# One transformer layer in float32 on one core: the first feed-forward product written out in seven slots, and parts of the output projection issued later

## The chip, the core and the metric

The kernel runs on one core of a Trainium2 chip. A core has five engines with an instruction stream each: TensorE (PE: matmuls, with a weight load of its own, PEld), VectorE (DVE), ScalarE (ACT), GpSimd (POOL) and SyncE (SP), which here issues the transfers to and from DRAM. The metric is device time in microseconds (us), the median of several runs. Each engine works through its own stream in order; semaphores hold an instruction until what it reads is written and what it overwrites has been read.

## The reference

One layer over x of 512 x 2048 float32: a norm, a combined projection to queries, keys and values, two kinds of attention with 8 heads each, an output projection, and a feed-forward block with 8192 hidden columns. Cut to what matters here:

```python
x = x + einsum('bse,ed->bsd', mixed, w_out)          # output projection
h2 = rmsnorm(x, g_mlp)
u = relu(einsum('bsd,df->bsf', h2, w_up))            # first feed-forward product
x = x + einsum('bsf,fd->bsd', u * u, w_down)         # second feed-forward product
return rmsnorm(x, g_final)
```

## The kernel before

**Two halves of a number.** A float32 operand is split into a high part that TensorE takes at full speed (fp32r) and a low part, the rest: ScalarE casts (L65, `CAST`), VectorE subtracts (L66). This pair is called a split here; `split` keeps the last of each as `casts` and `lows`. A matmul of two split operands takes three or four passes.

**Seven products in place of eight.** Each large product is cut into 2 x 2 blocks and done with seven block products, numbered 1 to 7, after Strassen and Winograd. The price is sums of blocks before a product (the parts of an operand, such as b22 - b12) and after it (the closes).

**Attention's end and the output projection (up to about 801 us).** `left(p, j)` splits part j of the left operand (the attention output `mixed`) for product p into `ah` and `al`, some parts with a sum on VectorE (L281 to L287). `split` with a scale does the values of attention, `vh` and `vl` (L68, L69). The last heads' probabilities are split into `ph` and `pl`. Products run in the order 1, 6, 2, 5, 3, 6 (last quarter), 7, 4, each in column halves c and steps j. The adds of their results into the residuals r are at L595. TensorE's order is written by hand from product 2 on; the other engines' order is made by a scheduler that goes by its own costs.

**The turn (about 780 to 830 us).** The results are transposed on TensorE (`turn_block`, the transposes at L681), scaled into `h`, summed and split into the seven forms fh1 to fh7 and fl1 to fl7 (`to_sum`, `to_high`, `to_low`).

**The first feed-forward product (about 801 to 1448 us).** It goes over 32 units of 256 hidden columns. A unit has seven products of sixteen matmuls: eight of 128x512 (L912) with the high part of the weights, eight of 128x256 (L914) with the low part, accumulated in three banks of PSUM, psa, psb and psc. Products 1, 6, 7 and 4 use psa, 2 uses psb, and 5 and 3 use psc. `split_part(p)` splits the weights of product p (`wu` to `wh` and `wl`). `close(p)` takes a result out: ScalarE copies psa to s (L925) for 1, 6 and 7 or to c (L941) for 4, and VectorE adds (L932 to L944). After product 3 ScalarE applies Relu and Square (L946, L947). Products of two units are interleaved: while unit u does 1, 5, 6, 2, 7, unit u - 1 ends with 4 and 3.

The weights' sums t1, t2, t3 (parts 5, 6 and 7) are for 20 of the 32 units made earlier in the program and stored in DRAM (`td`; the list `early`). The other 12 make their own: three sums of 128x1024 on VectorE (L890 to L893), from the raw weights. Part 4 always needs one more sum (L898).

**Stores.** Two units make a pair. When the odd one has its Square, the pair's seven parts for the second feed-forward product are made by `store_form`: for parts 5, 6, 7 and 3 a sum on VectorE (L661 to L667), then for each part a cast on ScalarE and a low on VectorE (`st`), then a store of 512 KB. Up to four are written per unit. The tiles of st rotate.

Of the kernel before, what the change touches and what calls it, by code (L numbers as in the profile page):

```python
# [8 lines left out]
F32 = mybir.dt.float32  # L9
# [31 lines left out]
def block_kernel(ctx, tc, x, g_attn, w_in, b_f, g_out_sb, g_out_fox, w_out, g_mlp, w_up, w_down, g_final, y):  # L41
# [18 lines left out]

    lows, casts, loads, scaled = [None], [None], [None], [None]

    def split(hi, lo, src, scale=None):
        if scale is None:
            ins = casts[0] = act.copy(hi, src)  # L65
            lows[0] = dve.tensor_tensor(lo, src, hi.bitcast(F32), op=ALU.subtract)  # L66
        else:
            ins = act.mul(hi, src, scale)  # L68
            scaled[0] = dve.scalar_tensor_tensor(lo, src, scale, hi.bitcast(F32), op0=ALU.mult, op1=ALU.subtract)  # L69
        return ins  # L70
# [138 lines left out]
    with tc.tile_pool(name="att", bufs=1, side="right") as at:  # L209
# [61 lines left out]
        def left_tile(p, pool_):  # L271
            LT[p] = tuple(pool_.tile([P, NH, 2 * P], F32R, tag=f"f{q}{LEFT_AT[p]}", name=f"a{q}{p}") for q in "hl")

        def left(p, j, k=1):

            m0, m1 = late["mixed"]
            ks = slice(2 * j, 2 * (j + k))
            a11, a21, a12, a22 = (m[:, ks, i:i + 2 * P] for m in (m0, m1) for i in (0, 2 * P))
            s = late["s"][j] if p in (5, 6, 3) else None
            if p == 5:  # L280
                dve.tensor_tensor(s, a21, a22, op=ALU.add)  # L281
            if p == 6:
                dve.tensor_tensor(s, s, a11, op=ALU.subtract)
# [213 lines left out]
        with tc.tile_pool(name="attp", bufs=1, space=PSUM) as atp:  # L497
# [58 lines left out]
            def before_outputs():  # L556
                late["mixed"] = [mixp.tile([P, NH, NT], F32, tag=f"x{i}", name="mixed") for i in range(2)]
                for k in range(2 * NH - 4):
                    load_mixed(k)
                left(1, 0)  # L560
                left(1, 1)

            def first_outputs():
# [11 lines left out]
                late["s"] = [w.rearrange("p (a b) -> p a b", a=2) for c in range(2) for w in two(c)]  # L575
# [185 lines left out]
    for c in range(2):  # L761
        for j in range(4):
            run_all(out_product(C[c], 5, c, [j], True, False))
            if j % 2:
                left(7, 2 * c + j // 2)
        add(r22[c], C[c])
# [43 lines left out]
    for j in range(4):  # L810
# [28 lines left out]
    class Unit:  # L839
        def __init__(self, u):  # L840
# [7 lines left out]

            def blocks():
                return rw.tile([P, 2, KC // 2, P], F32, tag="rw", name="wu")  # L850

            def wide(src):
                raw = rw.tile([P, KC // 2, 2 * P], F32, tag="rw", name="wu")
                sp.dma_start(raw, src)
                return [raw[:, :, j * P:(j + 1) * P] for j in range(2)]

            r, q = blocks(), blocks()
            b11, t2, t1, t3 = r[:, 0], r[:, 1], q[:, 0], q[:, 1]
            sp.dma_start(b11, first[:, :, :P])
            self.raw = u not in early  # L860
            if self.raw:
                sp.dma_start(t1, first[:, :, P:])
                sp.dma_start(t3, last[:, :, P:])
                sp.dma_start(t2, last[:, :, P:])
            else:
                for t_, j in ((t1, 0), (t2, 2), (t3, 1)):
                    sp.dma_start(t_, td[u][:, j])
            b21, b22 = wide(last)
            self.b = {1: b11, 5: t1, 6: t2, 2: b21, 7: t3, 3: b22, 4: b21}
            self.open_banks()  # L870

# [15 lines left out]
        def split_part(self, p):  # L887
            hi, lo = (w.rearrange("p (a b) -> p a b", b=P) for w in hi_lo(2 * NT))
            if p == 5 and self.raw:
                dve.tensor_tensor(self.b[7], self.b[7], self.b[5], op=ALU.subtract)  # L890
                dve.tensor_tensor(self.b[5], self.b[5], self.b[1], op=ALU.subtract)
            if p == 6 and self.raw:
                dve.tensor_tensor(self.b[6], self.b[6], self.b[5], op=ALU.subtract)  # L893
            if p == 4 and self.u < 2:
                dve.tensor_tensor(self.b[4], self.b[4], self.b[6], op=ALU.subtract)
            split(hi, lo, self.b[p])
            if p == 2 and self.u > 1:
                dve.tensor_tensor(self.b[4], self.b[4], self.b[6], op=ALU.subtract)  # L898
            self.parts[p] = hi, lo

        def product(self, p):
            if p not in self.parts:
                self.split_part(p)
            self.multiply(p)
            self.close(p)

        def multiply(self, p):
# [8 lines left out]
        def close(self, p):  # L916
# [26 lines left out]
            if p == 3:  # L943
                dve.tensor_tensor(self.m6, self.m6, self.C, op=ALU.add)  # L944
                sums(self.c[:, 1, t1], self.m6)
                act.activation(self.c, self.c, AF.Relu)  # L946
                act.activation(self.c, self.c, AF.Square)  # L947

# [101 lines left out]
    add(r21[0], A[0])  # L1050
    ahead[2] = out_piece(4, 1, 2)
    out_step(1)
    ahead[3] = out_piece(4, 1, 3)
    u0, u1 = Unit(0), Unit(1)
    u0.more(5)
    turn_block(1, 0, r21[0])
    to_sum(5, 0)
# [10 lines left out]
    u0.split_part(2)  # L1068
    u0.more(7)
    to_high(6, 0)  # L1070
# [13 lines left out]
    u1.split_part(1)  # L1084
    u1.more(5)
    for n in (1, 3):
# [25 lines left out]
    u1.multiply(2)  # L1112
    u0.split_part(7)
    for n in (0, 2):
# [5 lines left out]
    u0.multiply(5)  # L1120
    u1.split_part(5)
    both_cm.__exit__(None, None, None)
# [13 lines left out]
    u1.others()  # L1136
    for who, p in ((u0, 6), (u0, 7), (u1, 5), (u1, 6), (u0, 4), (u1, 7), (u0, 3)):
        who.product(p)
    more_parts.append(parts_hx)
    out_cm.__exit__(None, None, None)  # L1140
    old = u1
    for u in range(2, NU + 1):
        new = Unit(u) if u < NU else None
        if u == NU - 1:
            for p in ORDER:
                load_uf(p, GROUPS[0])
            b_first = load_b(GROUPS[0], 0)
        if new is None:
            second(1, b_first, 0, GROUPS[0][1], True)
        for i, (who, p) in enumerate(((new, 1), (old, 4), (new, 5), (new, 6), (old, 3), (new, 2), (new, 7))):  # L1150
            if who is None:
                continue
            who.product(p)
            if u == 3 and p == 6:
                v2 = cp.tile([P, TB], F32, name="v2")
                dve.tensor_reduce(v2, ss2, axis=mybir.AxisListType.X, op=ALU.add)
                dve.tensor_scalar(v2, v2, 1.0 / D, EPS, op0=ALU.mult, op1=ALU.add)
                ev = cp.tile([P, TB], F32, name="ev")
                dve.scalar_tensor_tensor(ev, v2, EPS, v2, op0=ALU.mult, op1=ALU.mult)
            if todo and u < NU - 1 and i in (0, 2, 4, 5):  # L1160
                store_form(*todo.pop(0))
            if p == 3 and who.u % 2 == 1 and who.u < NU - 2:
                todo += [(q, who.pair, who.u - 1) for q in A_ORDER]
        old = new
# [160 lines left out]
```

## Time and profile before

| | |
|---|---|
| time, median of 3 runs | 2074.25 us (2071.03 to 2074.33) |
| profiled execution | 2072.78 us, span 2071.1 us |
| TensorE busy | 2036.7 us, 98% |
| VectorE busy | 1656.5 us, 80% |
| ScalarE busy | 1074.2 us, 52% |
| mean granted TensorE clock | 0.996 |

A row of a time line gives the start, the duration, the engine, the line of the kernel, the operation with its tiles (written <- read) and shapes, and in brackets how long the engine had idled and what released it. A row of a group gives the count, then the busy time and the mean in ns, then the idle time before such instructions and what ended it. A row of the waits gives the total, the number and the longest. A row of the windows gives the busy time of each engine with its number of instructions, then the granted clock, the busy share of the DMA engines and GB/s. Busy times overlap: an instruction can start before the one ahead of it on its engine has ended, so the distance from start to start is what one costs in a row.

### The profile page before, as it was taken

How to read it: one execution, taken by the hardware profiler on the slowest of the kernel's cores; microseconds unless marked ns; L12 is line 12 of the kernel's file. 1: busy time of each engine (PE TensorE's matmuls, PEld its weight loads, DVE VectorE, ACT ScalarE, POOL GpSimd, SP SyncE). 2: the span in 40 equal slices, each digit the busy share in tenths (PEclk: the TensorE clock that was granted, in tenths of full speed). 3: DMA queues.
4: the chain of work that ended last, by engine and by line, in shares of the span. 5: the costliest groups of instructions: out<-in, count | busy, mean ns of one | idle time of the engine just before them, and what ended most of it. 6: DMA issues, size and time to landing. Idle time of an engine off the chain costs nothing.

```text
span 2071.1 us, 26773 instructions
## 1 busy us (share of the span) xinstructions
PE 2036.7 (98%) x10188; PEld 1729.7 (84%) x10188; DVE 1656.5 (80%) x1866; ACT 1074.2 (52%) x1419; POOL 69.7 (3%) x73
## 2 busy tenths in 40 slices
PE   9999999999999999999999999999999999999998
PEld 8888888888887888888888888888888888888886
DVE  4767767768777778888888888887899989888886
ACT  5334334444546566666666666655744434443433
POOL 0000000001102000000000000000000000000003
PEclk9999999999999999999999999999999999999999
DMA  7888878888754876776877777777865764764722
GB/s 242 270 292 280 287 251 272 287 274 265 254 187 140 257 231 197 255 251 232 268 247 241 257 261 254 235 248 261 293 244 215 268 242 159 267 236 131 269 93 102
DMA packets 371728, 492.60 MB, mean 238 GB/s; under 512 B 12760, under 2 KB 258568, under 8 KB 362512
## 3 DMA queue, kind: packets, MB, share of 16 engines
q1 hardware_dynamic: 370640, 488.77, 71.2%
q10 hardware_dynamic: 960, 2.13, 0.3%
q8 instruction: 80, 1.31, 0.2%
q14 instruction: 48, 0.39, 0.1%
HBM read 373.39 MB, written 117.46 MB: 237 GB/s over the span
## 4 chain that ended last, share of the span: by engine, by line
PE 88%; DVE 5%; DMA 3%; ACT 2%; issue 1%; SPq 0%; ACTq 0%; DVEq 0%
PE psa L912 9%; PE accd L99 8%; PE accd L98 8%; PE accd L100 8%; PE accq L98 5%; PE accq L99 5%; PE accq L100 5%; PE psa L914 5%; PE psc L912 5%; PE accv L98 3%; PE accv L99 3%; PE accv L100 3%; PE psc L914 2%; PE psb L912 2%; DMA ufd<-st 2%
## 5 line engine op out<-in xcount | busy, mean ns | idle before, releaser
L65 ACT CAST wh<-wraw 128x1024 fp32r<-128x1024 f32 (+2 forms) x157 | 160.8, 1026 | 241.8 <-PE accq L99 113.4
L66 DVE TENSOR_TENSOR wl<-wraw,wh 128x1024 fp32r<-128x1024 f32 (+2 forms) x157 | 186.7, 1191 | 101.0 <-ACT wh L65 100.7
L65 ACT CAST wh<-wu 128x1024 fp32r<-128x1024 f32 x160 | 166.9, 1049 | 116.4 <-PE psa L912 48.0
L65 ACT CAST wh<-wd 128x1024 fp32r<-128x1024 f32 (+1 forms) x134 | 132.6, 999 | 181.4 <-PE accd L100 125.0
L66 DVE TENSOR_TENSOR wl<-wu,wh 128x1024 fp32r<-128x1024 f32 x160 | 194.5, 1221 | 27.8 <-ACT wh L65 21.8
L98 PE MATMUL accq<-hH,wh 128*128 128x512 f32 x512 | 201.1, 393 | 0.0
L100 PE MATMUL accq<-hH,wl 128*128 128x512 f32 x512 | 199.8, 390 | 0.0
L99 PE MATMUL accq<-hL,wh 128*128 128x512 f32 x512 | 199.6, 390 | 0.0
L66 DVE TENSOR_TENSOR wl<-wd,wh 128x1024 fp32r<-128x1024 f32 (+1 forms) x134 | 153.1, 1153 | 34.9 <-ACT wh L65 34.7
L98 PE MATMUL accd<-wh,uf 128*128 128x512 f32 x428 | 166.5, 389 | 0.1
L100 PE MATMUL accd<-wh,uf 128*128 128x512 f32 x428 | 166.5, 389 | 0.0
L99 PE MATMUL accd<-wl,uf 128*128 128x512 f32 x428 | 166.5, 389 | 0.0
L65 ACT CAST wx<-wd 128x1024 fp32r<-128x1024 f32 (+1 forms) x90 | 89.5, 1001 | 118.3 <-PE accd L100 79.1
L66 DVE TENSOR_TENSOR wx<-wd,wx 128x1024 fp32r<-128x1024 f32 (+1 forms) x90 | 103.1, 1155 | 21.7 <-ACT wx L65 21.6
L99 PE MATMUL accd<-wx,uf 128*128 128x512 f32 x292 | 114.0, 390 | 0.5 <-DVE wx L66 0.3
L98 PE MATMUL accd<-wx,uf 128*128 128x512 f32 x292 | 113.6, 389 | 0.2 <-ACT wx L65 0.2
L100 PE MATMUL accd<-wx,uf 128*128 128x512 f32 x292 | 113.6, 389 | 0.0
L100 PEld LDWEIGHTS accq<-hH,wl 128*128 128x128 f32 x512 | 96.1, 188 | 20.1
L99 PEld LDWEIGHTS accq<-hL,wh 128*128 128x128 f32 x512 | 96.2, 188 | 19.0
L98 PEld LDWEIGHTS accq<-hH,wh 128*128 128x128 f32 x512 | 96.2, 188 | 18.9
L1020 DVE TENSOR_TENSOR m<-m,accd 128x1024 f32<-128x1024 f32 x84 | 102.2, 1217 | 11.1 <-PE accd L100 11.1
L912 PE MATMUL psa<-fh,wh 128*128 128x512 f32 x392 | 106.6, 394 | 0.7 <-ACT s L925 0.7
(307 smaller groups left out, 4845.4 us busy)
## 6 DMA issues: line engine op xcount, KB each, us to landing
ufd<-st SPq DMA_DIRECT2D x98, 512.0 KB, 5.4
wd<-in_w_down_dram SPq DMA_DIRECT2D x48, 1024.0 KB, 7.2
wraw<-in_w_in_dram SPq DMA_DIRECT2D x84, 512.0 KB, 5.8
uf<-ufd SPq DMA_DIRECT2D x42, 1024.0 KB, 6.6
wu<-in_w_up_dram SPq DMA_DIRECT2D x66, 512.0 KB, 6.8
wu<-in_w_up_dram SPq DMA_DIRECT2D x32, 1024.0 KB, 8.5
sums<-in_w_up_dram SPq DMA_DIRECT2D x60, 512.0 KB, 5.3
td<-sums SPq DMA_DIRECT2D x20, 1536.0 KB, 5.8
```

The lines of the kernel that those rows point to most:

```text
L65: ins = casts[0] = act.copy(hi, src)
L66: lows[0] = dve.tensor_tensor(lo, src, hi.bitcast(F32), op=ALU.subtract)
L98: pe.matmul(out, sh, mh, start=first, stop=False, skip_group_check=True)
L99: pe.matmul(out, sh, ml, start=False, stop=False, skip_group_check=True)
L100: pe.matmul(out, sl, mh, start=False, stop=last, skip_group_check=True)
L912: pe.matmul(ps, hi[:, a, :], both, start=a == 0 and p in (1, 2, 5), stop=False, skip_group_check=True)
L914: pe.matmul(ps[:, :2 * P], lo[:, a, :], F[p][a // 4][:, a % 4, 0, :], start=False, stop=a == KC // 2 - 1, skip_group_check=True)
L1020: dve.tensor_tensor(M[p][:, :, db, :], M[p][:, :, db, :], ps, op=ALU.add)
```

## The change

1. **The unit loop.** Its body is written out in seven slots, one for each product on TensorE, in the order new 1, new 5, old 4, new 6, old 3, new 2, new 7 (before, as written: new 1, old 4, new 5, new 6, old 3, new 2, new 7, with TensorE's order left to the scheduler). The order of ScalarE and VectorE is now the written one for units 2 to 30. Each split is written three slots ahead of its product.
2. **Stores.** In even steps one store form, in odd steps six.
3. **Own sums.** `early` is now every even unit and 1, 5, 21 and 31; again 20 units. The units that make their own sums are 3, 7, 9, 11, 13, 15, 17, 19, 23, 25, 27 and 29, so these sums stand in even steps, a unit ahead. The loads of a unit are three pieces (`load_r`, `load_q`, `load_wide`) in three of its slots.
4. **The output projection.** `left_after` issues a part after the last cast and the last low. The sums s of parts 0 and 1 are made earlier, and the other parts are spread over later steps. `left(1, 2, 2)` waits for both instructions of the last scaled split.
5. **The turn.** One more piece of product 4 goes ahead, the block's turn stands before `out_step(1)`, and the first units' products go 6, then unit 1's 5, then 7.

The number of instructions on each engine stays the same; their order and the rotation of their tiles differ.

The diff, cut to its core:

```diff
-    early = [u for u in range(NU) if u % 8 not in (2, 5, 7)]
+    early = [u for u in range(NU) if u % 2 == 0 or u in (1, 5, 21, 31)]
...
+        def left_after(*what):
+            with tc.issue_after(casts[0].ins), tc.issue_after(lows[0].ins):
+                left(*what)
...
-                with tc.issue_after(scaled[0].ins):
+                with tc.issue_after(scaled[0].ins), tc.issue_after(scaled[1].ins):
                     left(1, 2, 2)
...
-                        if c == 0 and j < 3:
-                            left(5, j)
-                            left(6, j)
+                        if j < 3:
+                            left_after(6 if c else 5, j)
...
-                        if c == 0 and j == 0:
-                            left(2, 0, 2)
-                        if c == 0 and j == 1:
-                            left(2, 2)
+                        if c == 1 and j == 0:
+                            left_after(2, 0, 2)
+                        if c == 1 and j == 1:
+                            left_after(2, 2)
...
-    ahead = {j: out_piece(4, 1, j) for j in range(2)}
+    ahead = {j: out_piece(4, 1, j) for j in range(3)}
...
+    FORMS = [(0, 1, 0, 0, 0, 0), (1, 1, 1, 1, 1, 1)]
...
+    rows_cm = tc.manual_schedule(engines={act.engine, dve.engine})
+    rows_cm.__enter__()
...
+    for u in range(2, NU - 1):
+        old, new = units_[u - 1], units_[u]
+        nxt = units_[u + 1] = Unit(u + 1)
+        odd = u % 2
+        nxt.load_r()
...
+        new.multiply(1)
+        if u > 2:
+            old.close(7)
+        store_next(FORMS[odd][0])
+        new.split_part(6)
+        new.multiply(5)
+        new.close(1)
+        old.split_part(3)
+        nxt.load_q()
+        store_next(FORMS[odd][1])
+        old.multiply(4)
+        new.split_part(2)
+        new.last_sum()
+        nxt.load_wide()
+        store_next(FORMS[odd][2])
+        new.multiply(6)
+        old.close(4)
+        new.split_part(7)
+        store_next(FORMS[odd][3])
+        old.multiply(3)
+        new.close(6)
+        nxt.split_part(1)
+        nxt.raw_sum(7)
+        store_next(FORMS[odd][4])
+        new.multiply(2)
+        old.close(3)
+        nxt.raw_sum(5)
+        nxt.split_part(5)
+        old.square()
+        store_next(FORMS[odd][5])
+        if old.u % 2 == 1 and old.u < NU - 2:
+            todo += [(q, old.pair, old.u - 1) for q in A_ORDER]
+        new.multiply(7)
+        new.close(2)
+        new.split_part(4)
+        nxt.raw_sum(6)
...
-    for u in range(2, NU + 1):
-        new = Unit(u) if u < NU else None
...
-        for i, (who, p) in enumerate(((new, 1), (old, 4), (new, 5), (new, 6), (old, 3), (new, 2), (new, 7))):
...
-            if todo and u < NU - 1 and i in (0, 2, 4, 5):
-                store_form(*todo.pop(0))
```

**VectorE at the end of attention.** w is an attention score tile (its scan is at L400 before and L404 after), al and wl are lows of the left parts and of the weights, vl the low of the values. Before, from the last scan to the fourth vl:

```order
L400 SCALAR_TENSOR_TENSOR w_5219<-w_5219 128x128
L66 TENSOR_TENSOR al5_5323<-r_5314,ah5_5322 128x512
L66 TENSOR_TENSOR al5_5323<-r_5315,ah5_5322 128x512
L401 TENSOR_TENSOR w_5219<-s_5206,w_5219 128x1280
L66 TENSOR_TENSOR wl_5396<-wraw_5393,wh_5395 128x1024
L66 TENSOR_TENSOR al5_5323<-r_5316,ah5_5322 128x512
L283 TENSOR_TENSOR r_5314<-r_5314,mixed_4989 128x512
L283 TENSOR_TENSOR r_5315<-r_5315,mixed_4989 128x512
L66 TENSOR_TENSOR al2_5321<-mixed_4990,ah2_5320 128x1024
L66 TENSOR_TENSOR al2_5321<-mixed_4990,ah2_5320 128x512
L69 SCALAR_TENSOR_TENSOR vl_5283<-accv_5012,r1v_563,vh_5282 128x256
```

With the change, from the third scan on:

```order
L404 SCALAR_TENSOR_TENSOR w_5225<-w_5225 128x512
L66 TENSOR_TENSOR al5_5325<-r_5011,ah5_5324 128x512
L404 SCALAR_TENSOR_TENSOR w_5225<-w_5225 128x128
L66 TENSOR_TENSOR wl_5390<-wraw_5387,wh_5389 128x1024
L285 TENSOR_TENSOR r_5013<-mixed_4989,mixed_4990 128x512
L69 SCALAR_TENSOR_TENSOR vl_5289<-accv_5018,r1v_563,vh_5288 128x256
```

Of the parts and sums that stood ahead of vl, one al and one sum are left; the rest, and w's next step, moved behind it. Further on stands the last head's pl, with the change:

```order
L388 SCALAR_TENSOR_TENSOR ph_5379<-ph_5379,ra_5378 128x512
L390 SCALAR_TENSOR_TENSOR mixed_4990<-os_5377,g_rest_83,ph_5379 128x512
L66 TENSOR_TENSOR wl_5577<-wraw_5574,wh_5576 128x1024
L601 TENSOR_TENSOR r_5316<-r_5316,acca_5310 128x512
L66 TENSOR_TENSOR pl_5488<-pt_5476,ph_5487 128x1280
```

A weight low and an add of product 1 stand right ahead of it; before, pl (reading pt_5482) came before the adds of the second column half.

**VectorE in the unit loop.** c is a pair's hidden tile, st a store's split, s a copied result, wu, wh and wl raw weights and their split. Before, around the stores of parts 5 and 6:

```order
L935 TENSOR_TENSOR s7_8118<-s7_8118,psc_7946 128x512
L661 TENSOR_TENSOR c_7712<-c_7712 128x2x256
L932 TENSOR_TENSOR c_8091<-s7_8118 128x256
L66 TENSOR_TENSOR wx_8288<-wu_8123,wx_8287 128x1024
L665 TENSOR_TENSOR c_7712<-c_7712 128x2x256
L66 TENSOR_TENSOR st_8203<-c_7712,st_8203 128x512
L66 TENSOR_TENSOR wl_8261<-wu_8128,wh_8260 128x1024
L942 TENSOR_TENSOR c_8091<-c_8091,psa_7947 128x256
L663 TENSOR_TENSOR c_7712<-c_7712 128x2x256
```

With the change, in an odd step:

```order
L667 TENSOR_TENSOR c_7749<-c_7749 128x2x256
L66 TENSOR_TENSOR st_8221<-c_7749,st_8221 128x512
L952 TENSOR_TENSOR c_8127<-c_8127,psa_7962 128x256
L66 TENSOR_TENSOR wx_8245<-wu_8009,wx_8244 128x1024
L669 TENSOR_TENSOR c_7749<-c_7749 128x2x256
L66 TENSOR_TENSOR st_8248<-c_7749,st_8248 128x512
L66 TENSOR_TENSOR wl_8272<-wu_8135,wh_8271 128x1024
L66 TENSOR_TENSOR st_8275<-c_7749,st_8275 128x512
L954 TENSOR_TENSOR s6_8079<-s6_8079,psc_7961 128x512
L942 TENSOR_TENSOR c_8127<-s6_8079 128x256
L66 TENSOR_TENSOR wl_8298<-wu_8191,wh_8297 128x1024
```

Before, a sum and the st low that follows from it had other work between them; now they stand one behind the other, as a close's two sums do.

**ScalarE in the same odd step, with the change:**

```order
L65 CAST st_8221<-c_7749 128x512
L951 COPY c_8127<-psa_7962 128x256
L65 CAST wx_8244<-wu_8009 128x1024
L65 CAST st_8248<-c_7749 128x512
L935 COPY s6_8269<-psa_8140 128x512
L65 CAST wh_8271<-wu_8135 128x1024
L65 CAST st_8275<-c_7749 128x512
L65 CAST wh_8297<-wu_8191 128x1024
L958 ACTIVATE c_8127<-c_8127 128x1024
```

Each cast stands in the row of its low above, with the copies of psa between them.

More of the change, by code (lines that the diff above doesn't have):

```diff
@@ L59, in block_kernel @@
     acc = acc_cm.__enter__()
-    lows, casts, loads, scaled = [None], [None], [None], [None]
+    lows, casts, loads, scaled = [None], [None], [None], []
     def split(hi, lo, src, scale=None):
@@ L561, in before_outputs @@
                 left(1, 1)
+                late["s"] = [w.rearrange("p (a b) -> p a b", a=2) for c in range(2) for w in two(c)]
+                for j in range(2):
+                    m0, m1 = late["mixed"]
+                    dve.tensor_tensor(late["s"][j], m0[:, 2 * j:2 * j + 2, 2 * P:], m1[:, 2 * j:2 * j + 2, 2 * P:], op=ALU.add)
             def first_outputs():
@@ L847, in __init__ @@
                 return
[L849 to L859, printed above, removed]
@@ new lines, in load_wide, with raw_sum @@
+        def load_wide(self):
+            raw = rw.tile([P, KC // 2, 2 * P], F32, tag="rw", name="wu")
+            u = self.u
+            sp.dma_start(raw, up_rows[1][:, :, 2 * u * P:2 * (u + 1) * P])
+            b21, b22 = (raw[:, :, j * P:(j + 1) * P] for j in range(2))
+            self.b.update({2: b21, 3: b22, 4: b21})
+        def raw_sum(self, p):
+            if self.raw:
+                a, b = {7: (7, 5), 5: (5, 1), 6: (6, 5)}[p]
+                dve.tensor_tensor(self.b[p], self.b[a], self.b[b], op=ALU.subtract)
@@ L905, in product @@
             self.close(p)
+            if p == 3:
+                self.square()
         def multiply(self, p):
@@ L945, in close, with square @@
                 sums(self.c[:, 1, t1], self.m6)
-                act.activation(self.c, self.c, AF.Relu)
-                act.activation(self.c, self.c, AF.Square)
+        def square(self):
+            act.activation(self.c, self.c, AF.Relu)
+            act.activation(self.c, self.c, AF.Square)
     def store_form(p, c, u):
@@ L1050, in block_kernel @@
     add(r21[0], A[0])
-    ahead[2] = out_piece(4, 1, 2)
+    ahead[3] = out_piece(4, 1, 3)
+    turn_block(1, 0, r21[0])
     out_step(1)
-    ahead[3] = out_piece(4, 1, 3)
     u0, u1 = Unit(0), Unit(1)
     u0.more(5)
-    turn_block(1, 0, r21[0])
     to_sum(5, 0)
@@ L1068, in block_kernel @@
     u0.split_part(2)
-    u0.more(7)
+    u1.more(5)
     to_high(6, 0)
@@ L1084, in block_kernel @@
     u1.split_part(1)
-    u1.more(5)
+    u0.more(7)
     for n in (1, 3):
@@ L1136, in block_kernel, with store_next @@
     u1.others()
-    for who, p in ((u0, 6), (u0, 7), (u1, 5), (u1, 6), (u0, 4), (u1, 7), (u0, 3)):
-        who.product(p)
-    more_parts.append(parts_hx)
+    def store_next(k=1):
+        for _ in range(k):
+            if todo:
+                store_form(*todo.pop(0))
+    FORMS = [(0, 1, 0, 0, 0, 0), (1, 1, 1, 1, 1, 1)]
+    units_ = {0: u0, 1: u1}
+    units_[2] = Unit(2)
+    u2 = units_[2]
+    for who, p in ((u0, 6), (u1, 5), (u0, 7), (u1, 6)):
+        who.product(p)
+    u2.load_r()
@@ new lines, in block_kernel @@
+    u0.last_sum()
+    u0.product(4)
+    u2.load_q()
+    u2.load_wide()
+    u1.product(7)
+    more_parts.append(parts_hx)
+    rows_cm = tc.manual_schedule(engines={act.engine, dve.engine})
+    rows_cm.__enter__()
+    u0.split_part(3)
+    u2.split_part(1)
+    u2.split_part(5)
+    u1.last_sum()
+    u0.multiply(3)
+    u1.split_part(4)
+    u0.close(3)
+    u0.square()
+    for u in range(2, NU - 1):
[4 more added lines that the diff above has]
+        if u > 2:
+            new.open_banks()
+        else:
+            u2.open_banks()
+        new.multiply(1)
+        if u > 2:
+            old.close(7)
[32 more added lines that the diff above has]
+        nxt.raw_sum(6)
+        if u == 3:
+            v2 = cp.tile([P, TB], F32, name="v2")
+            dve.tensor_reduce(v2, ss2, axis=mybir.AxisListType.X, op=ALU.add)
+            dve.tensor_scalar(v2, v2, 1.0 / D, EPS, op0=ALU.mult, op1=ALU.add)
+            ev = cp.tile([P, TB], F32, name="ev")
+            dve.scalar_tensor_tensor(ev, v2, EPS, v2, op0=ALU.mult, op1=ALU.mult)
@@ L1140, in block_kernel @@
+    rows_cm.__exit__(None, None, None)
     out_cm.__exit__(None, None, None)
-    old = u1
-    for u in range(2, NU + 1):
-        new = Unit(u) if u < NU else None
+    old = units_[NU - 2]
+    for u in range(NU - 1, NU + 1):
+        new = units_.get(u)
         if u == NU - 1:
+            new.open_banks()
             for p in ORDER:
@@ L1147, in block_kernel @@
             b_first = load_b(GROUPS[0], 0)
+            old.close(7)
         if new is None:
             second(1, b_first, 0, GROUPS[0][1], True)
-        for i, (who, p) in enumerate(((new, 1), (old, 4), (new, 5), (new, 6), (old, 3), (new, 2), (new, 7))):
+        for i, (who, p) in enumerate(((new, 1), (new, 5), (old, 4), (new, 6), (old, 3), (new, 2), (new, 7))):
             if who is None:
@@ L1153, in block_kernel @@
             who.product(p)
[L1154 to L1159, printed above, removed]
-            if todo and u < NU - 1 and i in (0, 2, 4, 5):
-                store_form(*todo.pop(0))
-            if p == 3 and who.u % 2 == 1 and who.u < NU - 2:
-                todo += [(q, who.pair, who.u - 1) for q in A_ORDER]
+            if who is new and p == 2:
+                new.last_sum()
         old = new
```

52 lines of the change are left out of this document (25 added, 27 removed).

## The prediction

> **What bounds the kernel now.** I read the page first, then TensorE's waits, then the time lines around the longest of them, and last the groups and windows of the stage that the change rewrites.
>
> ```profile
> span 2071.1 us, 26773 instructions
> ```
>
> The profiled execution took 2072.78 us, so 1.68 us lie around its span; the median of the runs shown, 2074.25, stands 0.07% above it. I sum against 2072.78. TensorE is busy for 98% of the span, so a gain can only come from its waits. They are few:
>
> ```profile
> PE psa L912 <- ACT s L925: 9.2, 6, 2.0
> PE o L100 <- DVE vl L69: 4.9, 1, 4.9
> PE psc L912 <- ACT wh L65: 1.8, 1, 1.8
> ```
>
> The first and third rows are the first feed-forward product (L912), the second is the end of attention. The time line of TensorE there:
>
> ```profile
> 640.21 0.48 PE L100 MATMUL o<-ph,vl 128*128 128x128 f32 x1 [4.85 <-DVE vl L69]
> ...
> 641.93 0.63 PE L98 MATMUL acca<-wh,ah 128*128 128x512 f32 x1
> 642.36 0.63 PE L99 MATMUL acca<-wl,ah 128*128 128x512 f32 x1
> ...
> 646.70 0.39 PE L98 MATMUL acca<-wh,ah 128*128 128x512 f32 x1
> 646.93 0.40 PE L99 MATMUL acca<-wl,ah 128*128 128x512 f32 x1
> ```
>
> The wait costs more than its 4.85 us: until 646.2 the matmuls start 0.43 us apart, afterwards 0.23. Fourteen of them lose 0.20 us each, 2.8 us. The other places, and two rows of the product's steady pace:
>
> ```profile
> 805.26 0.44 PE L681 MATMUL tr<-ident,r 128*128 128x128 f32 x2 [1.46 <-DVE r L595]
> ...
> 821.38 1.20 PE L912 MATMUL psa<-fh,wh 128*128 128x512 f32 x4 [0.68 <-ACT s L925]
> ...
> 1249.19 1.10 PE L912 MATMUL psb<-fh,wx 128*128 128x512 f32 x4
> ...
> 1288.28 1.09 PE L912 MATMUL psb<-fh,wh 128*128 128x512 f32 x4
> ...
> 1321.08 1.21 PE L912 MATMUL psa<-fh,wx 128*128 128x512 f32 x4 [1.96 <-ACT s L925]
> 1322.11 1.88 PE L912 MATMUL psa<-fl,wx 128*128 128x512 f32 x4
> 1323.79 1.06 PE L914 MATMUL psa<-fh,wx 128*128 128x256 f32 x4
> ```
>
> The two psb rows lie two units apart with no wait between: 39.09 us for a pair of units, fourteen products of 2.79 us. That is TensorE's own pace. After the wait of 1.96 us four matmuls take 1.68 us from start to start (1322.11 to 1323.79) and not 0.91; about 1.7 us go there. Inside the unit loop, then, the waits are 9.2 - 0.68 + 1.8 = 10.3 us, with the slow stretch 12.0.
>
> **The output projection and the turn.** VectorE between the third and the fourth vl before the wait:
>
> ```profile
> 629.47 3.04 DVE L400 TENSOR_TENSOR_SCAN w<-w 128x256 f32<-128x256 f32 x4
> 632.42 1.26 DVE L66 TENSOR_TENSOR al<-r,ah 128x512 fp32r<-128x512 f32 x2
> ...
> 635.01 1.21 DVE L66 TENSOR_TENSOR wl<-wraw,wh 128x1024 fp32r<-128x1024 f32 x1
> 636.14 0.68 DVE L66 TENSOR_TENSOR al<-r,ah 128x512 fp32r<-128x512 f32 x1
> 636.74 1.28 DVE L283 TENSOR_TENSOR r<-r,mixed 128x512 f32<-128x512 f32 x2
> ...
> 639.69 0.47 DVE L69 SCALAR_TENSOR_TENSOR vl<-accv,r1v,vh 128x256 fp32r<-128x256 f32 x1
> ```
>
> From 629.47 to 639.69 VectorE does 10.2 us of work. In the changed order only the four scans (2.95), one al (0.60), one weight low (1.13) and one sum of 128x512 (0.60) stand there: 5.3 us, so vl would start at 634.8 and end at 635.2. TensorE asked for it at 640.21 - 4.85 = 635.36. The wait goes, and the slow stretch with it: **-7.65**. Against it, the parts moved into the later steps now stand ahead of the last head's pl: in the changed order one weight low (1.13) and one add (0.60) right before it, and that head's product waits for pl. This costs between nothing (if TensorE arrives later still) and 1.73; since both run on the engine that is already the late one, I take 1.35. Net **-6.3**; bounds -7.7 and -5.9, and should the wait only move, 0.
>
> At 805 the transposes wait 1.46 for the last add of r21. The change puts one piece of the form earlier and the turn of the block ahead of that step, about 2 us less on VectorE before it: **-1.5** (0 if the add is late for another reason). At 821 unit 0's product 7 waited for the copy of product 6; now unit 1's product 5 stands between: **-0.8** (0.68 and a first matmul 0.16 late).
>
> **The unit loop.** This decides. ScalarE and VectorE stand in written order for units 2 to 30, and the written order hands work from one to the other. The prices of one instruction, in the loop:
>
> ```profile
> L66 DVE TENSOR_TENSOR wl<-wu,wh 128x1024 fp32r<-128x1024 f32 x160 | 194.5, 1221 | 27.8 <-ACT wh L65 21.8 <-issue 1.7 <-PE psa L914 1.6
> L66 DVE TENSOR_TENSOR st<-c,st 128x512 fp32r<-128x512 f32 x99 | 65.7, 686 | 17.4 <-ACT st L65 17.2
> ...
> L65 ACT CAST wh<-wu 128x1024 fp32r<-128x1024 f32 x159 | 165.9, 1049 | 113.8 <-PE psa L912 48.0 <-PE psc L912 22.0 <-PE psb L912 12.1
> L65 ACT CAST st<-c 128x512 fp32r<-128x512 f32 x99 | 58.5, 619 | 41.8 <-DMA ufd<-st 39.9 <-DVE c L663 1.5 <-DVE c L661 0.2
> L925 ACT COPY s<-psa 128x512 f32<-128x512 f32 x92 | 53.5, 582 | 12.9 <-DVE c L932 10.5 <-PE psa L914 2.3
> L946 ACT ACTIVATE c<-c 128x1024 f32<-128x1024 f32 x31 | 32.8, 1058 | 8.1 <-DVE c L932 7.8
> ```
>
> Back to back, VectorE's instructions start closer together than they last, and a dependent one does not:
>
> ```profile
> 953.30 0.68 DVE L944 TENSOR_TENSOR s<-s,psc 128x512 f32<-128x512 f32 x1
> 953.90 1.22 DVE L66 TENSOR_TENSOR wl<-wu,wh 128x1024 fp32r<-128x1024 f32 x1
> 955.04 0.69 DVE L667 TENSOR_TENSOR c<-c 128x512 f32<-128x512 f32 x1
> 955.64 0.42 DVE L932 TENSOR_TENSOR c<-s 128x256 f32<-128x256 f32 x1
> 955.98 0.68 DVE L66 TENSOR_TENSOR st<-c,st 128x512 fp32r<-128x512 f32 x1
> ...
> 959.81 1.23 DVE L66 TENSOR_TENSOR wx<-wu,wx 128x1024 fp32r<-128x1024 f32 x1 [1.08 <-ACT wx L65]
> ...
> 963.68 1.23 DVE L66 TENSOR_TENSOR wl<-wu,wh 128x1024 fp32r<-128x1024 f32 x1
> 964.94 1.22 DVE L898 TENSOR_TENSOR wu<-wu 128x1024 f32<-128x1024 f32 x1
> ```
>
> ```profile
> 958.75 1.03 ACT L65 CAST wx<-wu 128x1024 fp32r<-128x1024 f32 x1
> ```
>
> So 128x512 costs 0.60 (953.30 to 953.90), 128x1024 1.135, 128x256 0.34. A sum that reads or overwrites what the one before it used starts only when that has ended (963.68 + 1.23, and 0.03). A cast that ends at 959.78 releases its low at 959.81: a hand-over of 0.03.
>
> VectorE's work for a pair of units whose next odd unit makes its own sums: 14 lows, 2 last sums and 3 own sums of 128x1024, 19 x 1.135 = 21.6; 7 store lows and 4 store sums, 11 x 0.60 = 6.6; the closes, twice 3 x (0.60 + 0.34) + 0.33 = 6.3. Together 34.5 us of the 39.09. It would fit, if nothing idled. In the written order I count these holes in a pair:
>
> - Store parts 5, 6 and 3: sum, ScalarE's cast, low, with nothing of VectorE's between. 0.69 + 0.03 + 0.62 + 0.03 - 0.60 = 0.77 each, 2.3.
> - Store part 7 stands behind Relu and Square (two of 1.06, the second after the first); VectorE has one low and one sum meanwhile: 1.1.
> - The next unit's own sum 5, its cast, its low in a row: 1.22 + 0.03 + 1.05 + 0.03 - 1.135 = 1.2.
> - The cast of part 4 queued behind Relu and Square: 2.05 and 1.05 of ScalarE against 2.2 of VectorE: 0.8.
> - Casts queued behind copies and store casts (part 3, part 2, part 7, the next unit's part 1): 0.5, 0.35, 0.3 and 0.8, 2.0.
> - Eight sums that follow what they depend on (six closes, two last sums), 0.11 each: 0.9.
>
> Sum 8.3; the chain through VectorE and ScalarE lasts 34.5 + 8.3 = 42.75 us for a pair, 3.65 above TensorE's 39.09. In the order before, the scheduler had put two or three other instructions into most of these gaps; in the rows above st's lows idle only 17.4 us over 99.
>
> Twelve pairs are of this kind (next odd unit 3, 7 to 19, 23 to 29); where it is 5, 21 or 31 the three own sums and the hole of 1.2 are missing, 38.15, and nothing is lost. Splits are written three slots ahead, which lets one pair's lateness pass. So eleven pairs: 11 x 3.65 = 40.2. On top, the loads of the own sums:
>
> ```profile
> 982.51 0.38 SPq L862 DMA_DIRECT2D wu<-in_w_up_dram  x1
> ...
> 989.89 1.23 DVE L890 TENSOR_TENSOR wu<-wu 128x1024 f32<-128x1024 f32 x1 [0.92 <-DMA wu<-in_w_up_dram]
> ```
>
> From the issue to the sum pass 7.4 us; the changed order gives these loads some 7.2 from the low that frees their buffer. 0.15 for each of twelve: 1.8. So **+42** for the new waits, and **-12.0** for the old ones. On TensorE I expect them in every second unit from about unit 7: some 2.4 us before product 7 (psa waits for the copy of 6), 0.6 before old 4 and 0.8 before product 6.
>
> A wait of 1.96 us at 1321 was followed by slow matmuls, those of up to 1.75 were not. If 2.4 us always brings the slow stretch, 11 x 1.7 of slow matmuls arise; but VectorE's chain sets the pace and most of it only shortens the next waits: I put it at 0 to 4 and leave it out of the sum. The Trainium skill ("TensorE: Matmul & The Clock Gate", section "HAM oscillation — how this bites in real kernels") says that only idle gaps above some 3.4 us throttle; by it this term would be 0. The row at 1321 disagrees.
>
> **Sum.** 2072.78 - 6.3 - 1.5 - 0.8 - 12.0 + 42 = **2094.2 us**, 1.0% above the profiled execution.
>
> **Rivals.**
> (1) *The holes are covered.* If VectorE idles less than 39.09 - 34.5 = 4.6 us in a pair, there are no waits and the old ones are gone: 2072.78 - 20.6 = **2052**. It is slower than before from 4.6 + 20.6 / 11 = 6.5 us of holes on. For it: 2.8 us of my 8.3 are casts queued on ScalarE, counted without slack. Against: the store round trips, own sum 5, part 7 behind Square and the dependent sums, 5.5 us, follow from the order and the durations alone. Chance 0.14.
> (2) *Holes near 6.5*: 1.8 us of the queued casts hidden; the time stays at **2073**. 0.05.
> (3) *Transfers late.* In an odd step six stores and a next unit's six half-megabyte loads are 6.3 MB in some 20 us, 315 GB/s:
>
> ```profile
> 1230.00:1310.00 80.00, 80.00 (x460) 70.37 (x458) 69.98 (x90) 51.61 (x67) 0.00 (x0) 1.00 0.80 259
> ```
>
> At 259 GB/s the engines were 0.80 busy, so about 324 GB/s would fill them (an estimate). If the loads then land 1.2 us later, each of twelve pairs loses it again: 11 x 1.2 to the chain, **2107**; at 2 us, 2116. For it: the odd steps come within a few per cent of that limit. Against: even steps carry one store and drain the queue, and three slots lie between a store and the reuse of its buffer (8.4 us). Chance 0.16.
> (4) *The order is not the bound* and the waits before stay where they are, with the output part alone gained: 2072.78 - 8.6 = **2064**. The rows of the order speak against it, since TensorE's sequence itself changes. 0.03.
>
> **Chances and range.** The forecast (2085 to 2102, its own range) has 0.62. Slower: with (3) 0.78, and 0.01 from the upper end of (2), 0.79. Faster: (1) and (4), 0.17. The rest of (2), 0.04, lies within 0.2%, about 4 us and what a measurement of this kernel can tell from no change. The range for 8 in 10 reaches from 2066, which takes in (2), to 2114, which takes in most of (3); (1) and (4) lie outside.
>
> **What would show it.** The vl row of 4.85 us and the slow matmuls behind it gone, with a wait of 0 to 1.7 us on pl in its place; tr at about 805 without 1.46. In the loop, a psb row of the same unit parity 42 to 43 us after the last and not 39.09; psa waits from unit 7 on in every second unit, most of them for ACT s; none near units 5, 21 and 31; st lows of VectorE idling about 0.77 each on ACT st; VectorE busy less of each 80 us than the 69.98 above. I am wrong if the psb rows keep 39.1 (rival 1), and in the size if the own sums wait for DMA (rival 3).

## The result and the profile after

The changed kernel takes 2099.36 us (median of 4 runs, 2097.95 to 2101.89) against 2072.64 for the kernel before (4 runs, 2069.7 to 2074.33): a ratio of 1.0129, 95% interval 1.0113 to 1.0144. It is slower by 27 us. The prediction had 2094.2 and a range of 2066 to 2114.

The page of the changed kernel, its profiled execution (2097.95 us):

```profile
span 2096.2 us, 26721 instructions
```

TensorE's waits, of the whole kernel (us in total, times, longest):

```profile
PE psa L922 <- ACT s L935: 29.6, 26, 2.1
...
PE o L99 <- DVE pl L66: 1.4, 1, 1.4
```

The wait of 4.9 us on vl is gone, one of 1.4 on pl has come, and the waits on the copies of psa grew from 9.2 us in 6 to 29.6 in 26. TensorE's time line at the end of attention, and then at product 7 of every second unit:

```profile
635.02 0.33 PE L100 MATMUL o<-ph,vl 128*128 128x128 f32 x1
...
655.65 0.50 PE L99 MATMUL o<-pl,vh 128*128 128x512 f32 x1 [1.44 <-DVE pl L66]
...
948.76 1.20 PE L922 MATMUL psa<-fh,wx 128*128 128x512 f32 x4 [2.08 <-ACT s L935]
...
991.84 2.08 PE L922 MATMUL psa<-fh,wh 128*128 128x512 f32 x4 [2.08 <-ACT s L935]
...
1034.92 1.20 PE L922 MATMUL psa<-fh,wx 128*128 128x512 f32 x4 [2.08 <-ACT s L935]
...
1077.99 1.19 PE L922 MATMUL psa<-fh,wh 128*128 128x512 f32 x4 [2.09 <-ACT s L935]
```

From 948.76 to 991.84, 1034.92 and 1077.99 it is 43.08, 43.08 and 43.07 us: a pair of units now takes 43.1 us and not 39.1. VectorE's time line over one such pair, only the rows with a hole ahead of them:

```profile
1035.85 1.23 DVE L66 TENSOR_TENSOR wl<-wu,wh 128x1024 fp32r<-128x1024 f32 x1 [0.74 <-ACT wh L65]
...
1041.47 0.69 DVE L66 TENSOR_TENSOR st<-c,st 128x512 fp32r<-128x512 f32 x1 [0.99 <-ACT st L65]
...
1047.06 1.23 DVE L66 TENSOR_TENSOR wl<-wu,wh 128x1024 fp32r<-128x1024 f32 x1 [0.52 <-ACT wh L65]
...
1049.58 0.69 DVE L66 TENSOR_TENSOR st<-c,st 128x512 fp32r<-128x512 f32 x1 [0.69 <-ACT st L65]
1050.53 1.23 DVE L66 TENSOR_TENSOR wl<-wu,wh 128x1024 fp32r<-128x1024 f32 x1 [0.26 <-ACT wh L65]
...
1060.14 1.23 DVE L66 TENSOR_TENSOR wl<-wu,wh 128x1024 fp32r<-128x1024 f32 x1 [1.19 <-ACT wh L65]
...
1063.13 1.23 DVE L66 TENSOR_TENSOR wl<-wu,wh 128x1024 fp32r<-128x1024 f32 x1 [0.71 <-ACT wh L65]
...
1073.71 0.69 DVE L66 TENSOR_TENSOR st<-c,st 128x512 fp32r<-128x512 f32 x1 [0.69 <-ACT st L65]
...
1074.93 1.23 DVE L66 TENSOR_TENSOR wl<-wu,wh 128x1024 fp32r<-128x1024 f32 x1 [0.19 <-ACT wh L65]
...
1077.49 0.69 DVE L66 TENSOR_TENSOR st<-c,st 128x512 fp32r<-128x512 f32 x1 [0.73 <-ACT st L65]
```

Every hole ends with a cast of ScalarE; as the brackets count them, they are 6.7 us together. Where the next odd unit makes no own sums, the pace is TensorE's again. Around unit 21, psb:

```profile
1225.31 1.09 PE L922 MATMUL psb<-fh,wh 128*128 128x512 f32 x4
...
1244.86 1.09 PE L922 MATMUL psb<-fh,wh 128*128 128x512 f32 x4
...
1264.41 1.09 PE L922 MATMUL psb<-fh,wx 128*128 128x512 f32 x4
```

19.55 us a unit, 39.1 a pair. By stage, in the two profiled executions (the first matmul on psa begins the loop with its first units; the first accd that reads a wh follows its end):

| | before | after | difference |
|---|---|---|---|
| start to the first psa | 800.88 | 795.17 | -5.7 |
| first psa to first accd | 647.7 | 677.8 | +30.1 |
| first accd to the end | 622.5 | 623.3 | +0.8 |

### The profile page after: what moved, and what is told of

Read it like the earlier page. It is cut to its first block, busy times and chain, and to the rows that moved or that the text cites. A ratio compares the mean times of both kernels' runs of the same rounds, so it can differ in the third digit from the quotient of the medians.

```text
span 2096.2 us, 26721 instructions
## 1 busy us (share of the span) xinstructions
PE 2046.1 (98%) x10188; PEld 1733.4 (83%) x10188; DVE 1668.6 (80%) x1866; ACT 1069.1 (51%) x1419; POOL 59.7 (3%) x73
## 3 DMA queue, kind: packets, MB, share of 16 engines
q10 hardware_dynamic: 960, 2.13, 0.3%
## 5 line engine op out<-in xcount | busy, mean ns | idle before, releaser
L922 PE MATMUL psa<-fh,wh 128*128 128x512 f32 x392 | 111.7, 407 | 17.1 <-ACT s L935 16.9
L65 ACT CAST st<-c 128x512 fp32r<-128x512 f32 x105 | 64.7, 618 | 104.6 <-DVE c L667 47.9
```

The costliest lines, as they stand in the source:

```text
L922: pe.matmul(ps, hi[:, a, :], both, start=a == 0 and p in (1, 2, 5), stop=False, skip_group_check=True)
```

## The experiments

**Theory.** In the written order VectorE's next instruction often needs a cast that itself waits for VectorE's last one; the holes that this leaves make the two engines' chain longer than TensorE's 39.1 us for a pair. **Rivals.** The loss comes from the amounts and their place (six stores in one step, own sums in odd units only, the transfers that bunch); from the place of the copies in ScalarE's queue; or from the moved parts ahead of the loop.

In the table "loop" is the time from the first psa to the first accd in the profiled execution; ratios are to the kernel before, run beside on the same chip.

| | us | ratio (95%) | loop |
|---|---|---|---|
| before | 2072.64 | | 647.7 |
| the change | 2099.36 | 1.0129 (1.0113 to 1.0144) | 677.8 |
| 1 only what lies ahead of the loop | 2065.67 | 0.9951 (0.9937 to 0.9966) | 645.1 |
| 2 loop ordered by the scheduler | 2054.13 | 0.9900 (0.9885 to 0.9914) | 632.4 |
| 3 no own sums | 2054.56 | 0.9901 (0.9886 to 0.9916) | 633.0 |
| 4 store lows a slot late | 2131.71 | 1.0276 (1.0259 to 1.0294) | 709.8 |
| 5 store sums early | 2059.83 | 0.9928 (0.9911 to 0.9944) | 640.3 |
| 6 copy of product 6 earlier | 2100.45 | 1.0132 (1.0117 to 1.0147) | 679.4 |
| 7 only ScalarE in written order | 2072.44 | 0.9993 (0.9980 to 1.0006) | 649.6 |
| 8 only VectorE in written order | 2098.40 | 1.0122 (1.0107 to 1.0137) | 677.0 |
| 9 store sums and own sum 5 early | 2054.21 | 0.9910 (0.9893 to 0.9926) | 632.1 |
| 10 stores three and four | 2115.04 | 1.0204 (1.0189 to 1.0220) | 693.3 |

### 1. Only the parts ahead of the loop

The diff against the kernel before is that of the change up to the first two units (the output projection, the turn, u0's and u1's order); the loop is the old one.

> The kernel before with only the changes ahead of the unit loop (output projection's parts, the turn, the first two units' order); the loop is the old one. Theory (the loss lies wholly in the loop's written order): the first feed-forward product starts about 5.7 us earlier than before and the waits at 805 and 821 are gone, 8 us in all, so about 2064 to 2066. Rival (the moved parts leave the loop's engines later, and the loop's waits grow from that): 2075 or more.

2065.67 us, ratio 0.9951. The first psa starts at 795.45, 5.4 us earlier than before. This part of the change is a gain, 9.0 us by the medians of the runs side by side (2074.67 for the kernel before there): nothing of the loss comes from here.

### 2. The scheduler orders the loop again

```diff
-    rows_cm = tc.manual_schedule(engines={act.engine, dve.engine})
-    rows_cm.__enter__()
...
-    rows_cm.__exit__(None, None, None)
```

> The changed kernel, but ScalarE and VectorE in the unit loop ordered by the scheduler again; TensorE's order, the own sums in odd units, the six stores in odd steps as changed. Theory (holes in the written order of ScalarE and VectorE): a pair of units falls from 43.1 us to near 39.1, total 2055 to 2072. Rival (the amounts and their place: six stores in one step, own sums in odd units only, TensorE's order): stays above 2090.

2054.13 us, 0.9 below the range expected: 45 us less than with the written order, and 1.0% faster than the kernel before. The same instructions, six stores written in a step, own sums in odd units, TensorE's new order. TensorE's waits in the window 830 to 1460:

```profile
PE accd L98 <- ACT wx L65: 0.8, 2, 0.6
PE psa L922 <- ACT s L935: 0.4, 1, 0.4
```

The rival of the amounts falls: without the written order of ScalarE and VectorE the same amounts at the same places cost nothing. The loop is here 13 us shorter than in 1 (632.4 and 645.1 us), where it is the old one. Which of the loop's other changes (TensorE's order, the own sums' units, the stores' steps) brings this gain, no run separates.

### 3. No own sums

```diff
-                dve.tensor_tensor(self.b[p], self.b[a], self.b[b], op=ALU.subtract)
+                pass
```

This leaves out the three sums of the twelve units, and so changes what these units compute.

> The changed kernel without the three own sums of the twelve units that make them (that work is left out). Theory: VectorE's chain of a pair loses 3 x 1.135 and the hole of 1.2 behind sum 5, 43.1 - 4.6 = 38.5 us, below TensorE's 39.1, so no waits in the loop's pairs: 2054 to 2060. Rival (the copies out of psa are late because of their place behind casts in ScalarE's queue, whatever VectorE does): 2085 or more.

2054.56 us. The written order stands, VectorE has 3.4 us less to do in a pair and one hole of 1.2 less, and the waits are gone. In the window 830 to 1460 psa waits once:

```profile
PE psa L922 <- ACT s L935: 0.7, 1, 0.7
```

So the order by itself does not stop TensorE; the length of the chain against 39.1 us does.

### 4. Each store's low a slot later

```diff
+    def end_store():
+        if open_st:
+            p, u, st, src = open_st.pop(0)
+            dve.tensor_tensor(st[:, 1], src, st[:, 0].bitcast(F32), op=ALU.subtract)
+            send_store(p, u, st)
...
     def store_next(k=1):
+        end_store()
...
+            src = hidden_sum(p, c, c[:, :, 1, 2 * P:])
+            act.copy(st[:, 0], src)
+            open_st.append((p, u, st, src))
```

`hidden_sum` makes the store's sum, `send_store` issues its transfer; both are pieces of `store_form`.

> The changed kernel with each store's low written one slot after its cast; the same work. Theory: the holes in front of the store lows (0.73, 0.73, 0.69 and 0.99 in a pair) are filled, 43.1 - 3.1 = 40.0 us for a pair, 0.9 above TensorE's, total 2062 to 2074. Rival (ScalarE's queue or the copies' place sets the pace): 2090 or more. If it stays near 2085, the holes move behind other casts.

2131.71 us, 32 us slower than the change, where 25 to 37 us faster was expected. The time alone would suit the rival (2090 or more); VectorE's time line shows what happened:

```profile
1135.93 0.68 DVE L1159 TENSOR_TENSOR st<-c,st 128x512 fp32r<-128x512 f32 x1
1136.65 0.69 DVE L672 TENSOR_TENSOR c<-c 128x512 f32<-128x512 f32 x1
1139.51 1.22 DVE L66 TENSOR_TENSOR wl<-wu,wh 128x1024 fp32r<-128x1024 f32 x1 [2.16 <-ACT wh L65]
```

and ScalarE's:

```profile
1137.42 0.62 ACT L1168 CAST st<-c 128x512 fp32r<-128x512 f32 x1 [2.66 <-DVE c L672]
1137.95 0.58 ACT L938 COPY s<-psa 128x512 f32<-128x512 f32 x1
1138.42 1.05 ACT L65 CAST wh<-wu 128x1024 fp32r<-128x1024 f32 x1
```

The store lows wait for nothing any more (1135.93). But the round trip stays: from the start of the sum to the split's low behind it 2.86 us pass (1136.65 to 1139.51), and in the changed kernel 2.84 (1076.08 to 1078.92). There the store's own low stood inside this time; now it stands ahead of the sum, and VectorE idles for 2.16 us of the trip. The chain became longer by that: from this low of 1139.51 back to its like at 1094.06 it is 45.45 us, in place of 43.1. The sum has to come early, not the low late. ScalarE also waits for st tiles still being stored (33 us over the loop, in its groups: `DMA ufd<-st 33.4`), which it does not do in the changed kernel; the tiles are held longer here. How much of the 32 us is due to this, the run does not separate.

### 5. Each store's sum earlier

```diff
+        sum_next(FORMS[odd][3])
         new.split_part(7)
         store_next(FORMS[odd][3])
...
+        sum_next(FORMS[odd][5])
         nxt.split_part(5)
+        store_next(FORMS[odd][5])
         old.square()
-        store_next(FORMS[odd][5])
```

`sum_next` makes the sum of the slot's store; the other slots have it likewise, and in the third the store also stands ahead of part 4's last sum.

> The changed kernel, written order kept, with each store's sum ahead of the low of its slot's split instead of behind it, and the slot's store of part 7 ahead of Relu and Square; the same work. The store written a slot late ended slower because the sum came later and the next split's cast queued behind the store's cast. Theory, so amended (VectorE waits wherever its next instruction needs a cast that itself waits for VectorE's last one): the sum is done when ScalarE reaches the cast, and three holes of 0.7 and the one of 1.0 go; 43.1 - 3.1 = 40.0 us for a pair, total 2058 to 2072. Rival (the written order costs for another reason): 2090 or more.

2059.83 us. VectorE's group of store lows in the loop, in the changed kernel (830 to 1460 us) and here (830 to 1440):

```profile
L66 DVE TENSOR_TENSOR st<-c,st 128x512 fp32r<-128x512 f32 x98 | 67.6, 690 | 43.3 <-ACT st L65 43.3
```

```profile
L66 DVE TENSOR_TENSOR st<-c,st 128x512 fp32r<-128x512 f32 x100 | 68.5, 685 | 4.9 <-ACT st L65 4.8
```

38 us of holes are gone, and the loop is 37 us shorter. The pairs, at product 7:

```profile
1034.56 1.20 PE L925 MATMUL psa<-fh,wh 128*128 128x512 f32 x4 [1.57 <-ACT s L938]
...
1074.68 1.20 PE L925 MATMUL psa<-fh,wh 128*128 128x512 f32 x4 [0.72 <-ACT s L938]
...
1114.29 1.21 PE L925 MATMUL psa<-fh,wh 128*128 128x512 f32 x4 [0.24 <-ACT s L938]
```

40.1 and 39.6 us, where 40.0 was expected. VectorE's chain between 1034.06 and 1074.17 is 34.5 us of work, 4.6 of holes, counted from start to start, and 1.0 for sums that follow what they depend on: 40.1. The hole of 1.19 behind own sum 5 is still among them. Up to about 1000 us the pairs still take 39.1, and the waits at product 7 begin behind an own sum whose load came 2.13 us late (at 1004.08); so a part of the 8 us by which this loop is longer than that of 2 can belong to that load. The four runs lie between 2055.21 and 2062.08, and the profiled one is the slowest.

### 6. The copy that TensorE waits for, earlier in ScalarE's queue

```diff
         old.close(4)
+        new.close(6)
         new.split_part(7)
         store_next(FORMS[odd][3])
         old.multiply(3)
-        new.close(6)
```

> The changed kernel with the close of product 6 (ScalarE's copy out of psa, for which product 7 waits 2.08 us) written ahead of the split of part 7 and its store, one cast and one store cast earlier in ScalarE's queue. Theory (the period is set by VectorE's and ScalarE's chain, the copy is only where TensorE feels it): the pair stays at 42.5 to 43.5 us, total 2093 to 2104. Rival (the copy's place in the queue is the cause): the waits of 2.08 shrink by some 1.5 each, total 2075 to 2085.

2100.45 us, the same as the change. The wait moved from product 7 to another copy and kept its size:

```profile
1002.48 2.08 PE L922 MATMUL psa<-fh,wh 128*128 128x512 f32 x4 [2.21 <-ACT s L935]
...
1045.56 1.19 PE L922 MATMUL psa<-fh,wh 128*128 128x512 f32 x4 [2.18 <-ACT s L935]
```

The pair is 43.08 us, to the hundredth. The row that TensorE's wait names tells where lateness is felt, not where it is made.

### 7 and 8. One of the two engines in written order

```diff
-    rows_cm = tc.manual_schedule(engines={act.engine, dve.engine})
+    rows_cm = tc.manual_schedule(engines={act.engine})
```

and with `dve.engine` alone in the other.

> The changed kernel with only ScalarE in written order in the loop; VectorE's order is the scheduler's. Theory: VectorE's order decides, since a low right behind its sum's cast makes the hole; with other work moved between, 2054 to 2066. Rival (ScalarE's order decides: casts behind copies and behind Relu and Square): 2085 or more.

> The changed kernel with only VectorE in written order in the loop; ScalarE's order is the scheduler's. Theory: the holes that follow from VectorE's order alone stay (store round trips, own sum 5, dependent sums, about 5.5 us of a pair), those from ScalarE's queue shrink: a pair of 40 to 42.5 us, total 2065 to 2092. Rival (ScalarE's order decides): 2054 to 2062.

With ScalarE's order written and VectorE's free, 2072.44 us; with VectorE's written and ScalarE's free, 2098.40. Both lie outside what was expected, the first 6 us above its range, the second 6 above. ScalarE's order costs more than nothing (17 us above the scheduler's loop), and VectorE's costs all of it, though ScalarE's queue was free. In the second the holes are fewer and larger, VectorE's time line again:

```profile
1034.69 0.69 DVE L66 TENSOR_TENSOR st<-c,st 128x512 fp32r<-128x512 f32 x1 [2.73 <-ACT st L65]
1038.14 0.69 DVE L66 TENSOR_TENSOR st<-c,st 128x512 fp32r<-128x512 f32 x1 [0.69 <-ACT st L65]
...
1045.61 0.69 DVE L66 TENSOR_TENSOR st<-c,st 128x512 fp32r<-128x512 f32 x1 [2.25 <-ACT st L65]
...
1053.11 0.69 DVE L66 TENSOR_TENSOR st<-c,st 128x512 fp32r<-128x512 f32 x1 [0.69 <-ACT st L65]
...
1064.15 1.23 DVE L66 TENSOR_TENSOR wl<-wu,wh 128x1024 fp32r<-128x1024 f32 x1 [2.02 <-ACT wh L65]
```

8.4 us in this pair of 44.3 us; others are shorter, down to 41.8. ScalarE ahead of the first of these holes:

```profile
1032.52 1.05 ACT L65 CAST wh<-wu 128x1024 fp32r<-128x1024 f32 x1 [3.41 <-PE psa L922]
1033.55 0.59 ACT L935 COPY s<-psa 128x512 f32<-128x512 f32 x1
1034.03 0.62 ACT L65 CAST st<-c 128x512 fp32r<-128x512 f32 x1
```

The store's sum has ended at 1031.97, but the scheduler's ScalarE has a weight cast first, which waits for TensorE to release its tile, and a VectorE with a fixed order waits for the store's cast behind it. The two costs do not add up (17 and 45 against 45 together).

### 9. The own sum 5 earlier too

To the kernel of 5:

```diff
-        old.close(3)
         nxt.raw_sum(5)
+        old.close(3)
```

> The kernel with the sums early (2059.8 us, pairs of 39.6 to 40.1 us), and the own sum 5 one close earlier, so that its cast runs beside the close. Theory: the hole of 1.2 behind it shrinks to about 0.2, a pair's chain falls to about 38.8 us, below TensorE's 39.1; psa waits go, 2052 to 2057. Rival (the rest above the scheduler's order comes from something else than holes): unchanged, 2058 to 2062.

2054.21 us, as fast as the scheduler's order (2: 2054.13) and 0.9% faster than before. No psa wait is left in the loop; psb goes at TensorE's pace:

```profile
1020.96 1.09 PE L925 MATMUL psb<-fh,wh 128*128 128x512 f32 x4
...
1060.07 1.09 PE L925 MATMUL psb<-fh,wh 128*128 128x512 f32 x4
```

39.11 us. The low behind own sum 5 (at 1045.08) waits no more, after 1.19 us in 5. The gain on 5 is 5.6 us by the medians, with ratios whose intervals touch (0.9911 to 0.9944 and 0.9893 to 0.9926), and late loads can have a part in the time of 5. A written order was no worse here than the scheduled one once its chain fitted. Of the versions that keep all of the work, 2 and 9 are the fastest.

### 10. The stores spread evenly

```diff
-    FORMS = [(0, 1, 0, 0, 0, 0), (1, 1, 1, 1, 1, 1)]
+    FORMS = [(1, 1, 0, 1, 0, 0), (0, 1, 1, 1, 1, 0)]
```

> The changed kernel in written order with the stores spread as three in even and four in odd steps, in place of one and six; nothing else. Theory (holes per store, not the amount in a step): the pair stays between 42 and 44 us, total 2090 to 2106. Rival (six stores in one step, or the transfers bunched by them): 2080 or less.

2115.04 us, 9 above the range expected, and on the other side of the rival. A pair takes 44.36 us:

```profile
1017.36 1.19 PE L922 MATMUL psa<-fh,wh 128*128 128x512 f32 x4 [1.21 <-ACT s L935]
...
1061.72 1.20 PE L922 MATMUL psa<-fh,wh 128*128 128x512 f32 x4 [1.21 <-ACT s L935]
```

So six stores in one step are not at fault. The even spread makes the holes larger, with the same kinds among them: VectorE's time line has 7.8 us of them against 6.7 as the brackets count, 8.7 against 7.55 from start to start. A split's low right behind a store's low, for one, waits three times in a pair (0.74, 0.26 and 0.74 us), and twice in the changed kernel (0.26 and 0.74). 34.5 us of work, 8.7 and 1.2 for dependent sums are the 44.4 us of the pair.

## Why the prediction was right

Term by term, in the prediction's order; the loop's two terms are taken apart with the loop of experiment 2, which has next to no waits (632.4 us).

| term | predicted | measured |
|---|---|---|
| end of attention, pl's wait against it | -6.3 | -5.7 |
| transposes and unit 0's product 7 | -2.3 | -2.3 |
| old waits of the loop gone | -12.0 | -13.0 |
| new waits of the loop | +42 | +45.4 |
| behind the loop | 0 | +0.8 |
| sum (of unrounded times) | +21.4 | +25.1 |

- **The end of attention.** The matmul with vl starts at 635.02 instead of 640.21 and no slow stretch follows. The new wait on pl is 1.44 us, for which 1.35 was taken between bounds of 0 and 1.73. That it comes so close is luck: 1.35 was chosen and not worked out, and in the trace the weight low ahead of pl also waits 0.67 us for its cast (at 652.37), which the prediction did not have. A wait of 0.28 on al, not foreseen, is in the remaining 0.6.
- **The turn.** The waits at 805 and 821 are gone in the trace: 1.46 + 0.16 + 0.68 = 2.3 us.
- **The old waits.** 647.7 - 632.4 is 15.3 us for waits before, less the 2.3 of the turn: 13.0. This takes the loop of experiment 2 for the old loop without its waits.
- **The holes.** The prediction counted a hole from start to start, as the loss against instructions back to back. The brackets in the rows count from the end of the instruction before, and so leave out the overlap of some 0.09 us that a hole costs too. Counted as predicted, between the lows at 1035.85 and 1078.92:

| in a pair, from start to start | predicted | measured |
|---|---|---|
| 44 instructions back to back | 34.5 | 34.47 |
| before store lows | 3.4 | 3.43 |
| behind own sum 5 | 1.2 | 1.28 |
| behind Relu and Square | 0.8 | 0.80 |
| queued casts | 2.0 | 2.05 |
| dependent sums (0.92) and the rest | 0.9 | 1.05 |
| together | 42.75 | 43.07 |

  Each term of the chain is met within 0.2 us, so the mechanism was right in its parts. What was mis-sized is the loss that follows from them: a pair loses 43.07 - 39.11 = 4.0 us and up to 4.3, not 3.65, which for eleven pairs is 4 us and more, while the 1.8 us for late loads did not arise.
- **Where TensorE feels it.** Predicted 2.4 before product 7, 0.6 before old 4, 0.8 before product 6; measured 2.08, 0.37 and 0.59, from 938 us on. Where none was forecast there are three small ones: 0.28 and 0.36 at 867 and 876 us, and 0.67 at 1466, near unit 31.
- **Threshold.** Rival 1 said that without waits the time would be 2052, and that holes below 4.6 us do no harm. Experiments 2, 3 and 9 give 2054; 5, with pairs of 39.6 to 40.1, stands between.
- **The kinds of holes.** I had counted 5.5 us as fixed by order and durations and 2.8 as hanging on ScalarE's queue. Experiment 8 shows that this division does not hold: ScalarE free, the holes stay, elsewhere.
- **Transfers (rival 3).** The own sums wait 0.2 us for DMA over the whole loop, one split's low 0.7; the loads were not late. In the faster loops of 5 and 2 the own sums do wait for loads, 5.4 us over the loop in 5.
- **Slow matmuls.** Windows of four pairs of the changed kernel, from one wait of 2.08 to the next (length, busy time of the engines, granted clock, DMA share, GB/s):

```profile
948.76:991.84 43.08, 40.04 (x225) 34.64 (x225) 36.09 (x45) 25.30 (x34) 0.00 (x0) 1.00 0.72 232
991.84:1034.92 43.08, 41.01 (x224) 35.63 (x224) 36.09 (x45) 25.30 (x34) 0.00 (x0) 0.96 0.73 232
1034.92:1077.99 43.07, 40.98 (x224) 35.85 (x224) 36.09 (x45) 25.29 (x34) 0.00 (x0) 0.96 0.72 235
1077.99:1121.07 43.08, 40.03 (x225) 34.65 (x225) 36.10 (x45) 25.31 (x34) 0.00 (x0) 1.00 0.70 228
```

The second and third pair lose clock, the first and fourth do not, and all four are equally long. The slow matmuls cost nothing there, since VectorE's chain sets the pace; to leave them out of the sum was right for these pairs. In the slow pairs the small waits of 0.37 and 0.59 us are missing: the slow matmuls take the time in which TensorE would have waited. Two others take 43.34 and 43.39 at 0.96, so the price is 0 to 0.3 us for a pair. The Trainium skill ("TensorE: Matmul & The Clock Gate", section "HAM oscillation — how this bites in real kernels") names idle gaps above some 3.4 us as what throttles. The trace does not agree: the longest gap of TensorE in the changed kernel's loop is 2.09 us, and of the eleven waits of this size five were followed by slow matmuls (granted clock 0.66 or 0.67 in the 5 us behind them) and six were not (1.00).

## What to carry to other kernels

When two engines hand work to and fro in a written order, add up for each the instructions and the round trips of one period, from start to start: a busy share of 80% says nothing if the period with its holes is longer than that of the engine that should be the bound. Here the holes closed when what the other engine needs was made earlier (experiments 5 and 9), and not when its answer was read later (experiment 4). The instruction that the busiest engine waits for is where lateness shows; moving that instruction alone (experiment 6) moved the wait and left the period as it was.

## What was not expected

- Postponing a consumer by one slot cost 32 us (experiment 4): it stood ahead of the next producer and no longer within the round trip.
- Waits of TensorE of the same 2.08 us were followed by slow matmuls in five pairs and not in six (granted clock 0.96 and 1.00 above).
- Behind the loop the programs need from 622.5 us (before) to 625.7 (experiment 6) to the end, 623.3 with the change. It does not go with how early the loop ends: experiments 2 and 9, with short loops, have 624.6 and 624.8, experiments 6 and 8, with long ones, 625.7 and 625.2. Why it differs stays open.
